# Loading raw activations behind the store of their pair, and ordering their splits and sums behind the evictions

## The chip, the cores and the metric

The program runs on one core of one Trainium2 chip. The metric is the device time of a whole run in microseconds (us), from launch to the last output, taken as the median of several runs. The engines that matter are TensorE (PE in the rows: matrix multiplies; PEld: its weight loads), VectorE (DVE), ScalarE (ACT), GpSimd (POOL) and SyncE (SP, which here issues DMAs).

## The reference

One layer of a backbone with a state-space branch, a Fourier branch and a SwiGLU feed-forward stage, for 128 context tokens and 1024 latent tokens, all in float32. The change lies in the feed-forward stage alone:

```
h2 = rmsnorm(x, p["norm2_g"]) * (1.0 + scale2) + shift2
ff = (jax.nn.silu(h2 @ p["w_ffn_gate"]) * (h2 @ p["w_ffn_up"])) @ p["w_ffn_down"]
x = x + gate2 * ff
```

The model width D is 1024 and the hidden width 2816, which is 22 tiles of 128, taken as 11 pairs p = 0 to 10. The 1152 tokens are 9 tiles of 128.

## The kernel before

**Split products.** A float32 operand is held as two parts: a rounded copy (written by an ACT cast) and the rest (source minus rounded copy, by a two-input subtraction on POOL or DVE). A product of two such operands takes three matmuls for each 128-row step. `split` (L962, L963) does this for weights; `one` (L1294, L1295) does it for activations.

**Units of the gate and up projections.** `ffn_unit(p, "g" or "u", which)` multiplies the weights of one pair of hidden tiles with the tokens of sub-batch A (5 token tiles, 320 columns a matmul), B (4 tiles, 256 columns) or both, by a Strassen-Winograd scheme of seven products, in the order Z, W, X, Y, Z, X, Y. Each letter has one PSUM bank for each sub-batch, so a letter's second use needs the first to have been evicted. Evictions run on DVE (W at L1179, X at L1182 and L1193, Y at L1185 and L1197, into `ftA` and `fstB`) and ACT (Z at L1176, Silu at L1166); POOL makes the sums of weight blocks (L1172 to L1174, L1188) and multiplications (L1168). Tiles carry the unit in their names: `YAg7AB` is bank Y of sub-batch A in the gate unit of pair 7, `wh_u2AB` a split weight block of the up unit of pair 2.

**Order of the units.** Pair 0 is done first for sub-batch A only. Pairs 1 to 10 follow, gate then up, for both sub-batches. Behind pair 2 stand the two units of pair 0 for sub-batch B ("0B", `g0B` and `u0B`). Each weight unit loads two blocks of 512 KB, into a ring `ws` of three buffers. Only the gate weights of 0B, `ws_g0B` (L1126, L1127), go into another place: the pool `pgb` under the tag `gb`, which has a single buffer.

**Raw activations.** The end of an up unit stores the pair to device memory, `ffd` (L1207). For pairs 0 to 8 the 1024 latent tokens of it come back (L1278, two loads of 512 KB) as a tile `ra`, also with the tag `gb`. `a_steps(m)` turns `ra` into the seven operands P1 to P7 that the down projection wants: four sums on DVE (L1283) and seven splits (ACT L1294, DVE L1295) into a ring `stg` of three buffers, of which each is stored as `ad` (L1297). That is eleven operations of DVE and seven of ACT for each pair. They are passed as hooks, one for each product of the units of pair p = m + 1 (pair 10 for m = 0). The program order of the hooks is only a proposal: a scheduler orders the instructions of each engine by their dependences and modelled times.

**Down projection.** It runs in blocks, first m = 0 alone, then pairs of m. Block 0 starts with a tile `A1`, again with the tag `gb`, that holds P1 and P2 of m = 0 (L1358, loaded from `ad`); P6, P5 and P7 of m = 0 stay in `stg` and are not stored. The operands of block 1 (m = 1 and 2) are loaded ahead of block 0 for four of the seven products.

**Queues.** All these loads and stores are issued by SP in one order, and each waits there for its data and its buffer.

Of the kernel before, what the change touches and what calls it, by code (L numbers as in the profile page):

```python
# [10 lines left out]
F32 = mybir.dt.float32  # L11
F32R = mybir.dt.float32r
I32 = mybir.dt.int32
AF = mybir.ActivationFunctionType
ALU = mybir.AluOpType
# [4 lines left out]
NS = 1024  # L20
# [7 lines left out]
NF = FF // 128  # L28
G, P, H = 32, 64, 16
# [32 lines left out]
def tile_flow_step(ctx: ExitStack, tc: tile.TileContext, a, o):  # L62
    nc = tc.nc
    V, S, PL, PE, SY = nc.vector, nc.scalar, nc.gpsimd, nc.tensor, nc.sync
# [723 lines left out]
    for p in range(2):  # L788
        cs_ = slice(128 * p, 128 * p + 128)
        ev, od, oo, pp = mm_tile(f"ev{p}"), mm_tile(f"od{p}"), mm_tile(f"oo{p}"), aux_tile(f"fp{p}")  # L790
# [60 lines left out]
    for q in range(4):  # L851
# [3 lines left out]
                     func=AF.Gelu_apprx_tanh)  # L855
        S.activation(out=z32[:, q, NS:TOK].rearrange("p (c s) -> p s c", s=T), in_=zt[:, :, 0:CP],
                     func=AF.Gelu_apprx_tanh)
# [22 lines left out]
    pgb = open_pool("pgb", side="right")  # L880
# [74 lines left out]
    def weight_ws(src, name, n=1024):  # L955
        st = wr.tile([128, n], F32, tag="ws", bufs=NWS, name="ws_" + name)
        SY.dma_start(out=st, in_=src)
        return st
# [140 lines left out]
    ffd = dram.tile([NF, 128, TOK], F32, tag="ffd", name="ffd")  # L1099
    psF, fsl, tmp, last_st = {}, {}, {}, []  # L1100

    BORD = {"A": "YXWZ", "B": "ZWXY"}

    def open_sub(s, pools, tpool, tag=None):
        for z in "ZWXY":
# [9 lines left out]
        fsl[s] = fs_.rearrange("p (f t e c) -> p f t e c", f=2, t=nt, e=2)  # L1115
        tmp[s] = tm_.rearrange("p (v t c) -> p v t c", v=3, t=nt)

    def ffn_unit(p, kind, which, hooks=()):
        hooks = list(hooks)
        gate_ = kind == "g"  # L1120
        src = a["w_g"] if gate_ else a["w_u"]
        nm = f"{kind}{p}{which}"
        if nm == "g0B":
            gbw = pgb.tile([128, 2048], F32, tag="gb", name="ws_" + nm)
            w0, w1 = gbw[:, 0:1024], gbw[:, 1024:2048]
            SY.dma_start(out=w0, in_=src[0])  # L1126
            SY.dma_start(out=w1, in_=src[1])  # L1127
        else:
            w0 = weight_ws(src[2 * p], nm + "0")
            w1 = weight_ws(src[2 * p + 1], nm + "1")  # L1130
        a11, a12, a21, a22 = w0[:, 0:512], w0[:, 512:], w1[:, 0:512], w1[:, 512:]
        s1 = wr.tile([128, 512], F32, tag="S1", name="s1_" + nm)
        bk = {s: {z: psF[z + s].tile([128, 512], F32, tag=z + s, name=f"{z}{s}{nm}") for z in BORD[s]}
              for s in which}
        done = set()

        def le(i):
            return V if which == "B" or which == "A" and i % 2 == 0 else PL

        def product(w, tb, z):  # L1140
            for s in which:
                tv, nt, _ = subs[s]
                ps = bk[s][z][:, 0:64 * nt].rearrange("p (t c) -> p t c", c=64)
                first = (s, z) not in done
                done.add((s, z))
                for k in range(4):
                    ks = slice(128 * k, 128 * k + 128)
                    for i, (wv, tv_) in enumerate(((0, 0), (0, 1), (1, 0))):
                        PE.matmul(ps, w[:, wv, ks], tv[:, 0:nt, tv_, tb, k, :],
                                  start=(first and k == 0 and i == 0), stop=(k == 3 and i == 2),  # L1150
                                  skip_group_check=True)
            if hooks:
                hooks.pop(0)()

        def each(fn):
            for s in which:
                nt = subs[s][1]
                b = {z: t[:, 0:64 * nt].rearrange("p (t c) -> p t c", c=64) for z, t in bk[s].items()}
                fn(s, b, tmp[s], fsl[s])

        def put(fi, e, val):
            def go(s, b, t, fs):
                v = b[val] if isinstance(val, str) else t[:, val]
                dst = fs[:, fi, :, e, :]
                if gate_:
                    S.activation(out=dst, in_=v, func=AF.Silu)  # L1166
                else:
                    (V if isinstance(val, str) else PL).tensor_tensor(dst, dst, v, ALU.mult)  # L1168
            each(go)

        h = split(a11, nm + "a11", le(0))
        PL.tensor_tensor(s1, a21, a22, ALU.add)  # L1172
        PL.tensor_tensor(a21, a21, a11, ALU.subtract)
        PL.tensor_tensor(a11, s1, a11, ALU.subtract)  # L1174
        product(h, B11, "Z")
        each(lambda s, b, t, fs: S.copy(out=t[:, 0], in_=b["Z"]))  # L1176
        h = split(a11, nm + "s2", le(1))
        product(h, T2, "W")
        each(lambda s, b, t, fs: V.tensor_tensor(t[:, 0], t[:, 0], b["W"], ALU.add))  # L1179
        h = split(a21, nm + "s3", le(2))  # L1180
        product(h, T3, "X")
        each(lambda s, b, t, fs: V.tensor_tensor(t[:, 1], t[:, 0], b["X"], ALU.subtract))  # L1182
        h = split(s1, nm + "s1", le(3))
        product(h, T1, "Y")
        each(lambda s, b, t, fs: V.tensor_tensor(t[:, 1], t[:, 1], b["Y"], ALU.add))  # L1185
        put(1, 0, 1)
        h = split(a12, nm + "a12", le(4))
        PL.tensor_tensor(a12, a12, a11, ALU.subtract)  # L1188
        product(h, B21, "Z")
        put(0, 1, "Z")  # L1190
        h = split(a22, nm + "a22", le(5))
        product(h, T4, "X")
        each(lambda s, b, t, fs: V.tensor_tensor(t[:, 2], t[:, 0], b["X"], ALU.subtract))  # L1193
        put(1, 1, 2)
        h = split(a12, nm + "s4", le(6))
        product(h, B22, "Y")
        each(lambda s, b, t, fs: V.tensor_tensor(t[:, 0], t[:, 0], b["Y"], ALU.add))  # L1197
        put(0, 0, 0)
        if not gate_:
            for s in which:  # L1200
                _, nt, c0 = subs[s]
                st_ = dict(out=ffd[2 * p:2 * p + 2, :, c0:c0 + 128 * nt].rearrange("f p c -> p f c"),
                           in_=fsl[s].rearrange("p f t e c -> p f (t e c)"))
                if p == NF // 2 - 1:
                    last_st.append(st_)
                else:
                    SY.dma_start(**st_)  # L1207

    ps1 = open_pool("psF1", space=PSUM)
    pst_ = open_pool("psT", space=PSUM, side="right")  # L1210
# [35 lines left out]
    hk, no = h2_hooks(2), (lambda: None)  # L1246
# [14 lines left out]
    pst_.release()  # L1261
    ps2 = open_pool("psF2", space=PSUM)
    open_sub("B", {z: ps2 for z in "ZWXY"}, pm0, "m0a")
    KEYS = ("P1", "P2", "P6", "P5", "P7", "P4", "P3")
    LO, HI = slice(0, 512), slice(512, 1024)
    BLK = [[0]] + [[m, m + 1] for m in range(1, 9, 2)]
    STD = [9, 10]
    ad = {m: dram.tile([7, 128, 2, 512], F32, tag=f"ad{m}", name=f"ad{m}") for m in range(STD[0])}
    stg = pm0.tile([128, 3, 2, 512], F32R, tag="m0b", name="stg")
    nstg = 0  # L1270

    def a_steps(m):
        a_ = {}

        def start():
            raw = pgb.tile([128, 2, NS], F32, tag="gb", name=f"ra{m}")
            for f in range(2):
                SY.dma_start(out=raw[:, f], in_=ffd[2 * m + f][:, 0:NS])  # L1278
                for z, h in (("L", LO), ("H", HI)):
                    a_[f"{f}{z}"] = raw[:, f, h]  # L1280

        def comb(out, x, y, op=ALU.subtract):
            V.tensor_tensor(a_[out], a_[x], a_[y], op)  # L1283

        def p6():
            comb("0H", "0H", "1H", ALU.add)
            comb("0L", "0H", "0L")

        def one(ki):
            nonlocal nstg  # L1290
            src = a_[dict(P1="0L", P2="1L", P6="0L", P7="0L", P4="1H", P5="0H", P3="1L")[KEYS[ki]]]
            st_ = stg[:, nstg % 3]
            nstg += 1
            S.copy(out=st_[:, 0], in_=src)  # L1294
            V.tensor_tensor(st_[:, 1], src, f32(st_[:, 0]), ALU.subtract)  # L1295
            if m or ki not in (2, 3, 4):
                SY.dma_start(out=ad[m][ki], in_=f32(st_))  # L1297

        def do(*fs):
            return lambda: [one(f) if isinstance(f, int) else f() for f in fs]  # L1300

        p7a, p7b = (lambda: comb("1L", "1L", "0L")), (lambda: comb("0L", "1H", "0L"))
        return [no, no, start, no, no, no, do(0), do(1), do(5), p6, do(p7a, 6), do(2), do(3), do(p7b, 4)]

    for p in range(1, NF // 2):
        hk = a_steps((p - 1) % STD[0]) if p > 1 else [no] * 14
        ffn_unit(p, "g", "AB", hk[:7])
        ffn_unit(p, "u", "AB", hk[7:])
        if p == 2:
            ffn_unit(0, "g", "B")  # L1310
            ffn_unit(0, "u", "B")


    ps2.release()
# [35 lines left out]
    def load_at(m, ki):  # L1350
        key = KEYS[ki]
        if (m, key) in AT:
# [28 lines left out]
    def load_raw(m):  # L1381
        load_w(m)
        if m in STD:
            load_a(m)
# [10 lines left out]
    def prep(m, ki):  # L1395
        key = KEYS[ki]
        w0L, w0H, w1L, w1H = raws[m]
# [240 lines left out]
    for ki in range(7):  # L1638
        prep(0, ki)
    load_w(1)  # L1640
    for ki in range(4):
        for m in BLK[1]:
            load_at(m, ki)
    load_p(0)
# [123 lines left out]
```

## Time and profile before

| what | value |
|---|---|
| runs of the kernel before | 1544.62, 1551.46 and 1552.18 us, median 1551.46 |
| time of the profiled execution | 1544.15 us |
| its span from first to last instruction | 1542.4 us |
| mean granted clock of TensorE in it | 0.981 |
| busy: PE, DVE, ACT, POOL | 95%, 60%, 37%, 42% |
| DMA, mean over the span | 158 GB/s |

The shares of busy time are averages over stages with different limits; the feed-forward stage runs from about 694 us to the end, of which pairs 1 to 10 with 0B end at 1266.0 us. A window row gives the busy time of each engine in a stretch, then the granted clock of TensorE (1.00 is 2.4 GHz, 0.50 is 1.2 GHz), the mean share of the 16 DMA engines and their rate. In a timeline row the bracket tells how long the engine sat idle ahead of the instruction and what ended that.

### The profile page before, as it was taken

To read this page: it belongs to the slowest core of one execution; us is meant where nothing else is said; L and a number is where in the kernel's file an instruction comes from. 1 tells how busy PE (TensorE), PEld (TensorE's weight loads), DVE (VectorE), ACT (ScalarE), POOL (GpSimd) and SP (SyncE) were. 2 spreads that over 40 slices of the span, in tenths; PEclk is the share of its full clock that TensorE was granted. 3 is DMA by queue.
4 is the path that set the end of the run, shared out by engine and by line. 5 is a ranking of instruction groups with operands and counts; after the bars stand their busy time and mean duration, and the time that the engine had idled before them with its cause. 6 is when DMAs were issued, how large, how long until landed. Compare 5 with 4: busy or idle time off the path is not lost. (4 is left out here: it accounts for less than half of the span.)

```text
span 1542.4 us, 24033 instructions
## 1 busy us (share of the span) xinstructions
PE 1463.8 (95%) x8999; PEld 1312.6 (85%) x8999; DVE 928.8 (60%) x1838; ACT 565.0 (37%) x1096; POOL 648.9 (42%) x606
## 2 busy tenths in 40 slices
PE   6999999999999999988999999999999998999995
PEld 3799998899967778877689999999999996888774
DVE  4647989995264335379934544335454626667778
ACT  6523334343543122355543433233342334112323
POOL 4900000000132111455587587867677781322264
PEclk9999999999999999999899999999999999999998
DMA  8343233232525643454514444443544629666423
GB/s 317 110 130 96 75 109 115 74 105 101 171 76 197 201 145 110 152 203 165 191 69 161 167 173 176 148 158 147 209 181 154 236 102 392 228 219 225 143 69 123
DMA packets 101983, 243.83 MB, mean 158 GB/s; under 512 B 15710, under 2 KB 46047, under 8 KB 101868
## 3 DMA queue, kind: packets, MB, share of 16 engines
q1 hardware_dynamic: 101868, 242.30, 44.8%
q8 instruction: 71, 1.16, 0.3%
q14 instruction: 44, 0.36, 0.1%
HBM read 172.51 MB, written 69.74 MB: 157 GB/s over the span
## 5 line engine op out<-in xcount | busy, mean ns | idle before, releaser
L94 POOL TENSOR_TENSOR wh_glu<-ws_glu,wh_glu 128x512 fp32r<-128x512 f32 x4 | 5.1, 1275 | 338.4 <-ACT wh_glu L93 338.4
L271 PE MATMUL g<-h,wh_g 128*128 128x384 f32 (+1 forms) x432 | 147.3, 341 | 0.0
L272 PE MATMUL g<-h,wh_g 128*128 128x384 f32 (+1 forms) x432 | 147.1, 341 | 0.0
L273 PE MATMUL g<-h,wh_g 128*128 128x384 f32 (+1 forms) x432 | 146.3, 339 | 0.0
L1295 DVE TENSOR_TENSOR stg<-ra,stg 128x512 fp32r<-128x512 f32 x63 | 69.9, 1112 | 44.9 <-ACT stg L1294 44.9
L272 PEld LDWEIGHTS g<-h,wh_g 128*128 128x128 f32 x432 | 81.4, 188 | 0.2 <-issue 0.2
L271 PEld LDWEIGHTS g<-h,wh_g 128*128 128x128 f32 x432 | 81.2, 188 | 0.3 <-issue 0.3
L273 PEld LDWEIGHTS g<-h,wh_g 128*128 128x128 f32 x432 | 81.2, 188 | 0.2 <-issue 0.2
L1393 POOL TENSOR_TENSOR wd<-wd,wd 128x512 f32<-128x512 f32 x25 | 35.8, 1447 | 107.1 <-DMA wd<-in_w_d 57.7
L94 POOL TENSOR_TENSOR wh_pj<-ws_pj,wh_pj 128x512 fp32r<-128x512 f32 x16 | 22.1, 1380 | 104.3 <-ACT wh_pj L93 94.6
L1294 ACT CAST stg<-ra 128x512 fp32r<-128x512 f32 x63 | 38.1, 619 | 70.2 <-DMA ra<-ffd 47.2
L1446 DVE TENSOR_TENSOR acc<-acc,U 128x1024 f32<-128x1024 f32 x34 | 41.4, 1219 | 34.8 <-PE U L1427 34.5
L963 DVE TENSOR_TENSOR wh_out<-ws_out,wh_out 128x512 fp32r<-128x512 f32 x32 | 33.8, 1071 | 23.1 <-ACT wh_out L962 23.1
L1427 PE MATMUL q<-B,A 128*128 128x512 f32 x192 | 45.6, 393 | 0.6 <-DVE acc L1446 0.4
L1427 PEld LDWEIGHTS q<-B,A 128*128 128x128 f32 x192 | 35.8, 187 | 9.6 <-DVE acc L1446 0.8
L923 DVE TENSOR_TENSOR sgc<-sgc,p 128x384 f32<-128x384 f32 x24 | 13.3, 554 | 48.4 <-PE p L106 48.4
L963 POOL TENSOR_TENSOR wh_out<-ws_out,wh_out 128x512 fp32r<-128x512 f32 x16 | 22.4, 1406 | 47.2 <-ACT wh_out L962 41.9
L977 PE MATMUL o<-wh_out,m 128*128 128x512 f32 x96 | 37.0, 413 | 4.2 <-ACT scr0b L1059 4.2
L636 DVE TENSOR_TENSOR ta<-X,Sg 128x56 f32<-128x56 f32 (+10 forms) x88 | 39.2, 445 | 1.1
L639 DVE TENSOR_TENSOR X<-X,tb 128x56 f32<-128x56 f32 (+10 forms) x88 | 39.1, 453 | 0.9
L638 DVE TENSOR_TENSOR X<-X,ta 128x56 f32<-128x56 f32 (+10 forms) x88 | 38.8, 449 | 0.2
L637 DVE TENSOR_TENSOR tb<-X,Sg 128x56 f32<-128x56 f32 (+10 forms) x88 | 38.8, 441 | 0.0
(1638 smaller groups left out, 4479.5 us busy)
## 6 DMA issues: line engine op xcount, KB each, us to landing
ad<-stg SPq DMA_DIRECT2D x60, 512.0 KB, 2.6
A<-ad SPq DMA_DIRECT2D x60, 512.0 KB, 5.9
wa<-in_w_ada SPq DMA_DIRECT2D x48, 512.0 KB, 6.2
ws_out<-in_w_out SPq DMA_DIRECT2D x24, 512.0 KB, 4.1
wd<-in_w_d SPq DMA_DIRECT2D x22, 512.0 KB, 4.5
ind<-in SPq DMA_DIRECT2D x54, 192.0 KB, 1.9
ws_g<-in_w_in SPq DMA_DIRECT2D x18, 512.0 KB, 3.5
sgc<-ind SPq DMA_DIRECT2D x48, 192.0 KB, 3.2
```

The source lines that it names most:

```text
L271: PE.matmul(ps, w[:, 0, wsl], hi, start=first, stop=False)
L272: PE.matmul(ps, w[:, 0, wsl], lo, start=False, stop=False)
L273: PE.matmul(ps, w[:, 1, wsl], hi, start=False, stop=last)
L636: V.tensor_tensor(A, src, Sc[:, 0, lv, gs].unsqueeze(1).unsqueeze(3).to_broadcast(shp), ALU.mult)
L637: V.tensor_tensor(B, src, Sg[:, :, lv, gs].unsqueeze(3).to_broadcast(shp), ALU.mult)
L638: V.tensor_tensor(dst, dst, A, ALU.add)
L639: V.tensor_tensor(dst, dst, B[:, ::-1], ALU.add)
L963: (eng or PL).tensor_tensor(w[:, 1, :], src, f32(w[:, 0, :]), ALU.subtract)
L1294: S.copy(out=st_[:, 0], in_=src)
L1295: V.tensor_tensor(st_[:, 1], src, f32(st_[:, 0]), ALU.subtract)
L1427: PE.matmul(ps, A[:, va], B[:, vb], start=(first and ti == 0 and i == 0), stop=(last and ti == n - 1 and i == 2), skip_group_check=True)
L1446: V.tensor_tensor(dst, dst, ps, ALU.add)
```

## The change

Three things change. The load of `ra` stands in program order right behind the store of its pair, in `ffn_unit`, instead of in the third hook of the next gate unit; the second weight load of an up unit is ordered behind it. Where pair 2 is concerned, it stands behind 0B, and for m = 0 it stands behind pair 9. Every hook is ordered behind the last eviction of DVE and the last one of ACT that precede it in program order. And ahead of block 0 two products' operands of block 1 are loaded, not four.

```
+    def ra_load(m):
+        ra[m] = pgb.tile([128, 2, NS], F32, tag="gb", name=f"ra{m}")
+        for f in range(2):
+            i_ = SY.dma_start(out=ra[m][:, f], in_=ffd[2 * m + f][:, 0:NS]).ins
+        ra_ins[:] = [i_]
...
-            w1 = weight_ws(src[2 * p + 1], nm + "1")
+            with tc.issue_after(ra_ins[0]) if ra_ins and not gate_ else ExitStack():
+                w1 = weight_ws(src[2 * p + 1], nm + "1")
...
             if hooks:
-                hooks.pop(0)()
+                with ExitStack() as es:
+                    for i_ in ev.values() if p else ():
+                        es.enter_context(tc.issue_after(i_))
+                    hooks.pop(0)()
+
+        def ve(*x):
+            ev["V"] = V.tensor_tensor(*x).ins
+
+        def sc(**x):
+            ev["S"] = S.copy(**x).ins
...
                 else:
                     SY.dma_start(**st_)
+            if len(which) == 2 and p < STD[0] and p != 2:
+                ra_load(p)
...
-        def start():
-            raw = pgb.tile([128, 2, NS], F32, tag="gb", name=f"ra{m}")
-            for f in range(2):
-                SY.dma_start(out=raw[:, f], in_=ffd[2 * m + f][:, 0:NS])
...
-        return [no, no, start, no, no, no, do(0), do(1), do(5), p6, do(p7a, 6), do(2), do(3), do(p7b, 4)]
+        return [no, no, no, no, no, no, do(0), do(1), do(5), p6, do(p7a, 6), do(2), do(3), do(p7b, 4)]
...
             ffn_unit(0, "u", "B")
+            ra_load(2)
+        if p == NF // 2 - 2:
+            ra_load(0)
...
-    for ki in range(4):
+    for ki in range(2):
         for m in BLK[1]:
             load_at(m, ki)
```

The evictions of W, X and Y call `ve`, those of Z call `sc`, and Silu sets `ev["S"]`.

**DVE in the gate unit of pair 7.** Before (L1182, L1185, L1193 and L1197 are evictions, L1283 sums and L1295 splits of `ra`):

```order
L1182 TENSOR_TENSOR ftA<-ftA,XAg7AB 128x320
L1295 TENSOR_TENSOR stg<-ra_10914,stg 128x512
L1182 TENSOR_TENSOR fstB<-fstB,XBg7AB 128x256
L1283 TENSOR_TENSOR ra_10914<-ra_10914 128x512
L1295 TENSOR_TENSOR stg<-ra_10914,stg 128x512
L1283 TENSOR_TENSOR ra_10914<-ra_10914 128x512
L1295 TENSOR_TENSOR stg<-ra_10914,stg 128x512
L1185 TENSOR_TENSOR ftA<-ftA,YAg7AB 128x320
L1283 TENSOR_TENSOR ra_10914<-ra_10914 128x512
L1185 TENSOR_TENSOR fstB<-fstB,YBg7AB 128x256
```

Of the change, behind the last product of the gate unit (L1172 is now every eviction of W, X and Y, L1308 a split, L1296 a sum):

```order
L1172 TENSOR_TENSOR fstB<-fstB,YBg7AB 128x256
L1308 TENSOR_TENSOR stg<-ra_10813,stg 128x512 x2
L1172 TENSOR_TENSOR ftA<-ftA,WAu7AB 128x320
L1172 TENSOR_TENSOR fstB<-fstB,WBu7AB 128x256
L1296 TENSOR_TENSOR ra_10813<-ra_10813 128x512 x2
L1172 TENSOR_TENSOR ftA<-ftA,XAu7AB 128x320
L1172 TENSOR_TENSOR fstB<-fstB,XBu7AB 128x256
L1296 TENSOR_TENSOR ra_10813<-ra_10813 128x512
L1172 TENSOR_TENSOR ftA<-ftA,YAu7AB 128x320
L1308 TENSOR_TENSOR stg<-ra_10813,stg 128x512
L1172 TENSOR_TENSOR fstB<-fstB,YBu7AB 128x256
L1308 TENSOR_TENSOR stg<-ra_10813,stg 128x512 x2
```

The first split moved from between the first evictions of X in the gate unit to the place just ahead of that unit's last two evictions, which stand just ahead of this piece. The eleven operations now spread as far as the last product of the up unit, where the seventh split stands between that product's evictions of A and B. Behind the last row here comes the multiplication by the up product Z, which frees bank Z.

**SP around 0B.** Before (`ad_7684` is `ad` of m = 1, `ra_8248` is `ra` of m = 1):

```order
L1278 DMA ra_8248<-ffd 128x1024 x2
L957 DMA ws_u0B_8756<-in_w_u 128x1024
L1297 DMA ad_7684<-stg 128x1024 x7
L1126 DMA ws_g0B<-in_w_g 128x1024
L1127 DMA ws_g0B<-in_w_g 128x1024
L957 DMA ws_u0B_8758<-in_w_u 128x1024
L957 DMA ws_g3AB_8885<-in_w_g 128x1024
L1207 DMA ffd<-fsA 128x2x640
```

Of the change (`ra_8885` is `ra` of m = 2; `ffd<-fsA` at L1229 is the store of pair 2):

```order
L957 DMA ws_u0B_8758<-in_w_u 128x1024
L1310 DMA ad_7684<-stg 128x1024 x2
L957 DMA ws_g3AB_8888<-in_w_g 128x1024
L1310 DMA ad_7684<-stg 128x1024 x4
L1229 DMA ffd<-fsA 128x2x640
L1138 DMA ws_g0B<-in_w_g 128x1024
L1139 DMA ws_g0B<-in_w_g 128x1024
L1229 DMA ffd<-fstB 128x2x512
L1127 DMA ra_8885<-ffd 128x1024 x2
L957 DMA ws_g3AB_8890<-in_w_g 128x1024
```

The loads of `ws_g0B` stood ahead of the store of pair 2; they now stand behind it, and behind the store of the seventh split of m = 1.

**SP at the end of pair 10.** Before (`ad_7683` is `ad` of m = 0, `A_12751` is the tile `A1`, `wd` are weights of the down projection):

```order
L1278 DMA ra_12360<-ffd 128x1024 x2
L957 DMA ws_g10AB_12261<-in_w_g 128x1024
L1297 DMA ad_7683<-stg 128x1024 x2
L957 DMA ws_u10AB_12491<-in_w_u 128x1024
L1297 DMA ad_7683<-stg 128x1024 x2
L1358 DMA A_12751<-ad_7683 128x1024 x2
L1207 DMA ffd<-fsA 128x2x640
L1207 DMA ffd<-fstB 128x2x512
L957 DMA ws_u10AB_12493<-in_w_u 128x1024
L1378 DMA wd_12752<-in_w_d 128x1024
```

Of the change:

```order
L1127 DMA ra_12259<-ffd 128x1024
L1229 DMA ffd<-fstB 128x2x512
L957 DMA ws_u10AB_12493<-in_w_u 128x1024
L1394 DMA wd_12752<-in_w_d 128x1024
L1310 DMA ad_7683<-stg 128x1024
L1394 DMA wd_12754<-in_w_d 128x1024
L1310 DMA ad_7683<-stg 128x1024 x2
L1394 DMA wd_12787<-in_w_d 128x1024
L1310 DMA ad_7683<-stg 128x1024
L1374 DMA A_12751<-ad_7683 128x1024 x2
```

The load of `A1` stood ahead of the store of pair 9; it is now behind the weights of the down projection and the last store of m = 0, and its buffer is that of `ra` of m = 0, which is read up to the last split of pair 10.

## Rows read from the trace of the kernel before

**Rows 1.** The page: the span, and the first part, busy time.

```profile
span 1542.4 us, 24033 instructions
PE 1463.8 (95%) x8999; PEld 1312.6 (85%) x8999; DVE 928.8 (60%) x1838; ACT 565.0 (37%) x1096; POOL 648.9 (42%) x606
```

**Rows 2.** The waits of PE, 740 to 1266 us: total, times, longest.

```profile
PE YAg7AB L1149 <- DVE ftA L1185: 3.3, 1, 3.3
PE YAg9AB L1149 <- DVE ftA L1185: 2.4, 1, 2.4
PE YAg6AB L1149 <- DVE ftA L1185: 2.4, 1, 2.4
PE XAu9AB L1149 <- DVE ftA L1182: 2.0, 1, 2.0
PE YAg5AB L1149 <- DVE ftA L1185: 1.8, 1, 1.8
```

**Rows 3.** Windows: 0B with pair 3, then pairs 4, 7 and 10.

```profile
870.35:937.63 67.28, 64.95 (x506) 64.19 (x505) 31.13 (x53) 25.90 (x53) 53.03 (x45) 1.00 0.40 144
937.63:982.01 44.38, 44.38 (x338) 44.38 (x337) 19.27 (x33) 16.26 (x33) 30.50 (x25) 1.00 0.49 181
...
1075.42:1126.10 50.68, 47.34 (x338) 47.17 (x337) 20.41 (x33) 16.24 (x33) 37.27 (x32) 0.93 0.42 159
...
1221.59:1266.00 44.41, 44.41 (x339) 44.41 (x338) 11.18 (x26) 12.41 (x26) 37.97 (x35) 1.00 0.29 100
```

**Rows 4.** Timelines of SP, ACT, DVE and PE in the gate unit of pair 7.

```profile
1084.76 0.81 SPq L1278 DMA_DIRECT2D ra<-ffd  x2
...
1090.34 0.62 ACT L1294 CAST stg<-ra 128x512 fp32r<-128x512 f32 x1 [6.93 <-DMA ra<-ffd]
...
1090.99 1.51 DVE L1295 TENSOR_TENSOR stg<-ra,stg 128x512 fp32r<-128x512 f32 x1 [6.72 <-ACT stg L1294]
...
1097.31 0.47 DVE L1185 TENSOR_TENSOR ftA<-ftA,YAg7AB 128x320 f32<-128x320 f32 x1
...
1097.93 3.54 PE L1149 MATMUL YAg7AB<-TA,wh_g7ABs 128*128 128x320 f32 x12 [3.34 <-DVE ftA L1185]
```

**Rows 5.** Windows behind that wait, and around another wait of PE.

```profile
1097.90:1101.50 3.60, 3.57 (x14) 3.60 (x15) 2.71 (x5) 3.43 (x8) 0.40 (x1) 0.50 0.61 245
...
685.40:689.55 4.15, 0.00 (x0) 0.00 (x0) 4.15 (x8) 0.51 (x2) 1.44 (x1) 0.76 0.09 20
689.55:693.90 4.35, 4.35 (x10) 3.47 (x11) 4.35 (x10) 1.76 (x4) 2.98 (x3) 0.50 0.56 222
```

**Rows 6.** Timelines of SP, ACT, POOL and PE around the start of 0B.

```profile
851.21 0.45 SPq L1126 DMA_DIRECT2D ws_g0B<-in_w_g  x1
...
855.81 0.62 ACT L962 CAST wh_g0Ba<-ws_g0B 128x512 fp32r<-128x512 f32 x1 [1.53 <-DMA ws_g0B<-in_w_g]
...
862.29 1.15 ACT L962 CAST wh_g0Bs<-ws_g0B 128x512 fp32r<-128x512 f32 x2 [5.86 <-POOL ws_g0B L1174]
...
857.08 1.29 POOL L1172 TENSOR_TENSOR s_g0B<-ws_g0B 128x512 f32<-128x512 f32 x1 [2.21 <-DMA ws_g0B<-in_w_g]
...
871.75 1.56 PE L1149 MATMUL WBg0B<-TB,wh_g0Bs 128*128 128x256 f32 x12
```

**Rows 7.** Timelines of SP and POOL: one weight load of 512 KB.

```profile
1108.80 0.33 SPq L957 DMA_DIRECT2D ws_g8AB<-in_w_g  x1
...
1112.36 1.29 POOL L1172 TENSOR_TENSOR s_g8AB<-ws_g8AB 128x512 f32<-128x512 f32 x1 [2.33 <-DMA ws_g8AB<-in_w_g]
```

**Rows 8.** Timeline of PE in blocks 0 and 1.

```profile
1265.99 2.97 PE L1427 MATMUL U<-B0P,A 128*128 128x512 f32 x12
...
1298.64 0.50 PE L1427 MATMUL Y<-B1P,A 128*128 128x512 f32 x1 [1.21 <-ACT B1P L1346]
```

**Rows 9.** A window at the start of the down projection.

```profile
1266.00:1286.00 20.00, 19.63 (x86) 15.59 (x84) 8.09 (x8) 8.88 (x11) 5.20 (x5) 1.00 1.00 372
```

**Rows 10.** The tile stg: its splits on DVE (ns, minimum, median, maximum), its stores.

```profile
L1295 DVE TENSOR_TENSOR stg<-ra,stg x63: 676/694/1794, 837.1 to 1219.3; 128x512 fp32r<-128x512 f32 x63
...
DMA to landing us min/median/max: 2.6/2.6/3.9
```

More of the change, by code (lines that the diff above doesn't have):

```diff
@@ L1102, in tile_flow_step @@
     BORD = {"A": "YXWZ", "B": "ZWXY"}
+    ev, ra, ra_ins = {}, {}, []
     def open_sub(s, pools, tpool, tag=None):
@@ L1116, in open_sub @@
         tmp[s] = tm_.rearrange("p (v t c) -> p v t c", v=3, t=nt)
+    KEYS = ("P1", "P2", "P6", "P5", "P7", "P4", "P3")
+    LO, HI = slice(0, 512), slice(512, 1024)
+    BLK = [[0]] + [[m, m + 1] for m in range(1, 9, 2)]
+    STD = [9, 10]
+    def ra_load(m):
[3 more added lines that the diff above has]
+        ra_ins[:] = [i_]
     def ffn_unit(p, kind, which, hooks=()):
@@ L1165, in go @@
                 if gate_:
-                    S.activation(out=dst, in_=v, func=AF.Silu)
+                    ev["S"] = S.activation(out=dst, in_=v, func=AF.Silu).ins
                 else:
@@ L1175, in ffn_unit @@
         product(h, B11, "Z")
-        each(lambda s, b, t, fs: S.copy(out=t[:, 0], in_=b["Z"]))
+        each(lambda s, b, t, fs: sc(out=t[:, 0], in_=b["Z"]))
         h = split(a11, nm + "s2", le(1))
         product(h, T2, "W")
-        each(lambda s, b, t, fs: V.tensor_tensor(t[:, 0], t[:, 0], b["W"], ALU.add))
+        each(lambda s, b, t, fs: ve(t[:, 0], t[:, 0], b["W"], ALU.add))
         h = split(a21, nm + "s3", le(2))
         product(h, T3, "X")
-        each(lambda s, b, t, fs: V.tensor_tensor(t[:, 1], t[:, 0], b["X"], ALU.subtract))
+        each(lambda s, b, t, fs: ve(t[:, 1], t[:, 0], b["X"], ALU.subtract))
         h = split(s1, nm + "s1", le(3))
         product(h, T1, "Y")
-        each(lambda s, b, t, fs: V.tensor_tensor(t[:, 1], t[:, 1], b["Y"], ALU.add))
+        each(lambda s, b, t, fs: ve(t[:, 1], t[:, 1], b["Y"], ALU.add))
         put(1, 0, 1)
@@ L1192, in ffn_unit @@
         product(h, T4, "X")
-        each(lambda s, b, t, fs: V.tensor_tensor(t[:, 2], t[:, 0], b["X"], ALU.subtract))
+        each(lambda s, b, t, fs: ve(t[:, 2], t[:, 0], b["X"], ALU.subtract))
         put(1, 1, 2)
@@ L1196, in ffn_unit @@
         product(h, B22, "Y")
-        each(lambda s, b, t, fs: V.tensor_tensor(t[:, 0], t[:, 0], b["Y"], ALU.add))
+        each(lambda s, b, t, fs: ve(t[:, 0], t[:, 0], b["Y"], ALU.add))
         put(0, 0, 0)
@@ L1263, in tile_flow_step @@
     open_sub("B", {z: ps2 for z in "ZWXY"}, pm0, "m0a")
[L1264 to L1267, printed above, removed]
     ad = {m: dram.tile([7, 128, 2, 512], F32, tag=f"ad{m}", name=f"ad{m}") for m in range(STD[0])}
@@ L1272, in a_steps @@
     def a_steps(m):
-        a_ = {}
-        def start():
-            raw = pgb.tile([128, 2, NS], F32, tag="gb", name=f"ra{m}")
-            for f in range(2):
-                SY.dma_start(out=raw[:, f], in_=ffd[2 * m + f][:, 0:NS])
-                for z, h in (("L", LO), ("H", HI)):
-                    a_[f"{f}{z}"] = raw[:, f, h]
+        a_ = {f"{f}{z}": ra[m][:, f, h] for f in range(2) for z, h in (("L", LO), ("H", HI))}
         def comb(out, x, y, op=ALU.subtract):
```

## The prediction

> **What bounds the kernel now.** The page says that PE is busy 95% of the span [rows 1]. So the question is not who is slow on average but where PE stands still. For the feed-forward stage I read the list of PE's waits first: in pairs 5 to 9 it waits for DVE's eviction of a bank, 1.8 to 3.3 us each time, 11.9 us in five waits [rows 2]. Then the windows, pair by pair: pair 4 has no wait and takes 44.38 us, in which PE is busy throughout; pair 7 takes 50.68 us at a granted clock of 0.93 [rows 3]. The reader is to see that 44.38 us is the floor of a pair, and that a wait costs more than its length. Pair 7 lies 6.3 us above the floor, but its wait is 3.34 us. The rest is clock: right behind the wait the granted clock is 0.50, which is 1.2 GHz, and elsewhere 4.15 us without a matmul are followed by 4.35 us at 0.50 [rows 5]. At half the clock 4.35 us do the work of 2.2, so a restart costs 2.2 to 3.0 us on top of the idle time.
>
> Then the timeline, to see why DVE was late in pair 7 [rows 4]. SP issues the raw load at 1084.76; the first cast finds its data at 1090.34; DVE, idle for 6.72 us, starts the first split at 1090.99. Three sums and three splits have been put between the first X evictions and the Y eviction, which therefore comes at 1097.31. PE wanted that bank 3.34 us before 1097.93. DVE was idle first and then had everything at once.
>
> **What the change takes away.** From 937.63 to 1266.00 there are seven pairs in 328.37 us [rows 3]. Seven floors are 7 x 44.38 = 310.7. The excess is 17.7 us, and it consists of these waits and the slow clock behind them. In the new order no split stands between evictions that a next product waits for until the gate unit's sixth product is evicted, and the load is issued a whole gate unit earlier, so it has landed. I take the 17.7 us as gone, with 12 as the lower end, if one or two waits stay.
>
> Does DVE keep up? The densest place is the up unit. A product takes 44.38 / 14 = 3.17 us, an eviction at most 0.47 [rows 4], a split between 0.68 and 1.79 [rows 10]. I take the worst, 1.77 each. Behind product W come two evictions and two sums, 0.94 + 3.54 = 4.48 us, so DVE is 1.3 us late at X. Behind X: 1.3 + 0.94 + 1.77 = 4.0, so 0.85 late at Y. Behind Y an eviction, a split, an eviction, two splits: 0.85 + 0.94 + 5.3 = 7.1 us after Y's end. The multiplication that frees bank Z starts then and ends some 7.6 us after Y's end. The next unit wants that bank three products after Y's end, at 9.5. About 2 us are left, at the worst price of every operation; so the cost here is nothing.
>
> A rule speaks against this. The Trainium skill (GPSIMD Engine Reference, Specifications) lists GpSimd's SBUF interfaces as shared with VectorE, with contention for VectorE instructions that have two SBUF inputs; splits and sums are of that kind, and they move beside POOL's work. The trace agrees, since one shape takes 676 to 1794 ns [rows 10]. By the rule all eleven would pay, which is the case worked out above, and it still fits; the rule's own outcome is the second rival.
>
> The up unit's second weight load now stands behind two raw loads of 512 KB. At 372 GB/s [rows 9] these take 2.8 us. It is wanted at the start of the up unit, half a pair (22 us) later, so I cost it at nothing; without that cover it would be 2.8 us a pair.
>
> **First loss: the start of 0B.** The gate weights of 0B share the single buffer with the raw activations. Before, all splits of m = 1 were early, the load was issued at 851.21, and 0B started at 870.35 without a wait [rows 3, 6]. Now the seventh split of m = 1 stands behind the A eviction of the last product of the up unit of pair 2. Call the end of that unit E. The A half of the last product ends 1.4 us before E; an eviction of 0.47 and a split of 0.7 to 1.8 put the release of the buffer at E - 0.2 to E + 0.9, and I take E + 0.4. SP then still issues the store of that split and the store of pair 2 ahead, some 0.4 us each (0.45 for one issue, [rows 6]), so the load is issued at E + 1.3. From issue to the first cast took 4.6 us, from issue to the first POOL sum 5.87 [rows 6]. So product Z starts at about E + 6.7, and POOL starts its three sums at E + 7.2, which are 3.9 us at 1.29 each. A cast of 0.6 and a little for the semaphores follow, and W starts at E + 11.9. Before, it started at 871.75, which is E + 1.4. Behind W thirteen products of B remain, at 1.40 each (871.75 - 870.35), which is 18.2. With 2.5 us for the slow clock, 0B ends at E + 32.6, and pair 3 adds 44.4: 77.0 us against 67.28 [rows 3]. The 67.28 held 3.2 us over the floor of 64.1 (44.38 x 4/9 for 0B, and 44.38); that goes too, since pair 3's weights have time enough. **Loss 9.7 us.** If the load lands in 3.56 us, as an undisturbed one did [rows 7], and SP has nothing ahead, it is about 5 to 6; if the buffer comes free late by a further 3 us, 13.
>
> **Second loss: block 0.** P1 and P2 of m = 0 come through the tile A1. Before, its load was long done and block 0 followed without a wait at 1265.99 [rows 8]. Now it waits for the last split of pair 10, by the same working 0.4 to 0.9 us after the end T of that pair. A load takes 3.56 us [rows 7], so the first matmul starts at about T + 4.2, and the restart costs 2.6. Some comes back: in block 1 PE waits for operands anyway, 1.21 us once [rows 8], at a time when the DMA engines are full [rows 9], and a later PE waits less for them. On the other side 1 MB of A1 now falls into that full time (2.8 us at 372 GB/s), while 2 MB of block 1's operands move out of it. I give back 1.5 us. **Loss 5.3 us**, 3 to 8. Loading two products ahead, not four, is a part of this term alone.
>
> **The sum** is -17.7 + 9.7 + 5.3 = -2.7 us. The profiled execution took 1544.15 us (span 1542.4, [rows 1], and 1.75 around it), so the same execution comes to 1541.4. But of the three runs of before one lies at that level and two lie 7 to 8 us above it; the median is 7.3 above the profiled time. Where the median of three runs of the changed kernel falls is open by that much. I take the middle, 1541.4 + 3.6 = **1545.0 us**, which is 0.4% below 1551.46. A measurement of this kernel can tell about 0.5%, 7.8 us, from no change: faster is below 1543.7, slower above 1559.2.
>
> **The rivals.**
> First, **cheap restarts**: the two new waits lie at their lower ends, 5.5 and 3. That is -17.7 + 8.5 = -9.2, and 1538.5 us by the same middle. For it: the 3.56 us of an idle queue [rows 7]. Against: at 0B three POOL sums stand in a row.
> Second, on the other side, **DVE too late after all**: the three splits behind Y in the up unit need a free buffer of the ring of three, and a store takes 2.6 us to land [rows 10]. If each of the last two waits for such a store, the bunch grows by more than the 2 us that are left, and PE waits at the start of each of the nine units that follow, some 2 us. It decides from 2 us on. That gives -2.7 + 18 = +15.3, 1563 us. The rule of the Trainium skill on shared interfaces (GPSIMD Engine Reference, Specifications) points the same way, since it makes the splits the longest exactly where they are bunched. Against: DVE at the worst price still fits.
> Third, **dear restarts**: 13 and 8 at the two places, -17.7 + 21 = +3.3, 1551 us, no change.
> Fourth, **the change does not do what it says**: the raw loads come no earlier, since SP is in order and something ahead of them waits, and the splits end as late as ever. Then the 17.7 us stay and the losses come on top: +15, 1563 us. Against: the store of the pair is all that stands ahead of the load.
>
> **How the numbers follow.** Chances: the forecast 0.50, cheap restarts 0.20, dear restarts 0.17, DVE too late 0.08, no earlier load 0.05. Because of the two levels of the runs, a little under half of the forecast's chance (0.22) falls below 1543.7, and nearly all of cheap restarts (0.19): faster 0.41. Slower are the second and fourth rival but for a little, 0.11. The rest, 0.48, is the same. The range 1533 to 1556 holds the forecast, the cheap and the dear restarts at either level of the runs but for their ends, and leaves out the two slow rivals.
>
> **What would show it.** Right: no wait for `ftA` or `fstB` in the gate units of pairs 5 to 9, each of pairs 4 to 10 close to 44.4 us; a gap of PE of about 6.7 us ahead of `ZBg0B` and one of 4 to 5 ahead of `WBg0B`, with a granted clock of 0.50 behind; 0B and pair 3 together at about 77 us from the end of the last Y product of pair 2; a gap of about 4 us ahead of the first U of block 0. Wrong: waits at bank Z at the start of the units behind each pair's splits; a gap ahead of `ZBg0B` under 3 or over 10 us; a raw load that is issued in the gate unit's third product or later; or waits on weights in the up units, which I have costed at nothing.

## The result and the profile after

The changed kernel is slower. Five runs of it took 1560.15 to 1564.09 us (median 1561.44), five of before 1544.62 to 1552.18 (median 1548.83): a ratio of 1.0082, with a 95% interval of 1.0059 to 1.0105. The forecast was 1545.0 with a range of 1533 to 1556, so the time lies outside it, on the side to which I gave 0.11.

The profiled execution of the changed kernel took 1564.09 us, with a span of 1562.3 (before: 1542.4, [rows 1]). Its stages come out of the start times of PE's first matmuls. E is the end of pair 2, T the end of pair 10, each of them the start of the next matmul less PE's wait for it:

| stage (us) | before | after | difference | forecast |
|---|---|---|---|---|
| start to E | 870.35 | 873.89 | +3.5 | 0 |
| 0B and pair 3 | 67.28 | 78.59 | +11.3 | +9.7 |
| pairs 4 to 10 | 328.37 | 317.99 | -10.4 | -17.7 |
| T to the end | 276.41 | 291.83 | +15.4 | +5.3 |

The first line is no effect of the change: 3.4 us of it lie ahead of pair 1 (which begins at 778.20 and 781.57), where the instructions of each engine stand in the same order in both kernels, and that stage varies from run to run (last section). The other three lines add up to +16.3. The medians differ by 12.6; the profiled execution of after is the slowest of its five, and that of before is at the low end of its runs.

The waits of PE in the changed kernel from 600 to 1300 us (total, times, longest), those of the stages in question:

```profile
PE U L1443 <- DMA A<-ad: 10.2, 1, 10.2
PE ZBg0B L1162 <- ACT wh_g0Ba L962: 7.6, 1, 7.6
...
PE WBg0B L1162 <- ACT wh_g0Bs L962: 2.4, 1, 2.4
...
PE WAu7AB L1162 <- POOL wh_u7ABs L963: 0.8, 1, 0.8
PE WAu8AB L1162 <- POOL wh_u8ABs L963: 0.8, 1, 0.8
...
PE WAu8AB L1162 <- ACT wh_u8ABs L962: 0.7, 1, 0.7
PE WAu7AB L1162 <- ACT wh_u7ABs L962: 0.6, 1, 0.6
```

All five waits on `ftA` of [rows 2] are gone, as forecast. In their place stand the two gaps that I had priced, at 0B and ahead of block 0, and a third kind that I had costed at nothing: product W of the up units of pairs 7 and 8 waits for split weights.

The windows of the changed kernel: 0B with pair 3, pairs 7 and 8, the gap ahead of block 0, and what follows it.

```profile
873.89:952.48 78.59, 68.12 (x506) 67.15 (x505) 37.69 (x58) 29.12 (x58) 57.37 (x46) 0.93 0.39 136
...
1086.20:1132.60 46.40, 44.99 (x336) 44.50 (x337) 21.02 (x34) 15.94 (x35) 36.02 (x29) 1.00 0.47 173
1132.60:1180.65 48.05, 46.51 (x338) 46.05 (x337) 22.44 (x37) 17.10 (x36) 37.45 (x31) 0.96 0.47 178
...
1270.47:1280.68 10.21, 0.01 (x1) 0.03 (x1) 4.61 (x9) 2.19 (x5) 9.40 (x10) 0.67 0.25 87
1280.68:1286.00 5.32, 5.32 (x16) 4.28 (x17) 0.00 (x0) 2.27 (x3) 3.11 (x3) 0.67 1.00 393
```

Pair 8 is 3.7 us above its floor of 44.38 with waits of 1.5; its clock is 0.96, so the rest is again the restart. In the gap ahead of block 0 POOL is busy for 9.40 of 10.21 us. POOL had no part in the forecast of that gap, so this is the first sign that something else is late there.

**The gap at 0B.** SP, ACT, PE and POOL in the changed kernel (timelines):

```profile
873.65 0.32 SPq L1310 DMA_DIRECT2D ad<-stg  x1
874.38 0.37 SPq L1229 DMA_DIRECT2D ffd<-fsA  x1
874.80 0.51 SPq L1138 DMA_DIRECT2D ws_g0B<-in_w_g  x1
...
880.84 0.62 ACT L962 CAST wh_g0Ba<-ws_g0B 128x512 fp32r<-128x512 f32 x1 [8.35 <-DMA ws_g0B<-in_w_g]
...
881.51 3.29 PE L1162 MATMUL ZBg0B<-TB,wh_g0Ba 128*128 128x256 f32 x12 [7.62 <-ACT wh_g0Ba L962]
887.17 0.50 PE L1162 MATMUL WBg0B<-TB,wh_g0Bs 128*128 128x256 f32 x2 [2.38 <-ACT wh_g0Bs L962]
```

It is the chain of the forecast, link by link: the store of the seventh split, the store of pair 2, then the load, issued at E + 0.9 (forecast E + 1.3); Z at E + 7.6 (6.7) and W at E + 13.3 (11.9). The load took 6.0 us from issue to the first cast, where the row I used had 4.6 [rows 6].

**The up weights.** SP, POOL and PE around the up unit of pair 7, which begins its product Z at 1108.46:

```profile
1097.36 0.37 SPq L1229 DMA_DIRECT2D ffd<-fstB  x1
1100.46 0.83 SPq L1127 DMA_DIRECT2D ra<-ffd  x2
1101.38 0.38 SPq L957 DMA_DIRECT2D ws_u7AB<-in_w_u  x1
...
1107.68 1.29 POOL L1194 TENSOR_TENSOR s_u7AB<-ws_u7AB 128x512 f32<-128x512 f32 x1 [6.59 <-DMA ws_u7AB<-in_w_u]
...
1112.41 0.56 PE L1162 MATMUL WAu7AB<-TA,wh_u7ABs 128*128 128x320 f32 x2 [0.62 <-ACT wh_u7ABs L962]
```

Read from above: the raw load can't start before the store of its pair has landed, 3.1 us after its issue; the up weights follow the raw load, and land 6.3 us later; three POOL sums, a cast and a split follow. Pair 7 began at 1086.20, so the weights were issued 15.2 us into a pair that wants them split 25 us into it. Before, the same load was issued 7.8 us into pair 7, which began at 1075.42, and the raw load of [rows 4] 2.8 us after the store that it reads back. SP before:

```profile
1081.99 0.38 SPq L1207 DMA_DIRECT2D ffd<-fstB  x1
1083.24 0.35 SPq L957 DMA_DIRECT2D ws_u7AB<-in_w_u  x1
```

**The gap ahead of block 0.** The chain that ended last in the changed kernel, 1258 to 1281 us (start, length, what):

```profile
1258.53 5.98 DMA ad<-stg
...
1265.13 0.61 ACT stg L1307
...
1273.06 1.60 POOL wd L1409
1274.68 0.05 ACT B0P L1362
...
1275.82 0.53 ACT stg L1307
1276.37 0.82 DVE stg L1308
1277.22 3.32 DMA A<-ad
...
1280.68 4.62 PE U L1443 x12
```

The last link is the one I forecast: the load of A1 is issued when the last split has freed the buffer, and lands 3.3 us later. But that split ends at 1277.19, which is T + 6.7, not T + 0.4 to 0.9. ACT has one order, and ahead of the last cast of `stg` stand casts of the down weights, which wait for POOL's sums of them. ACT's timeline has two waits, the first for a store that frees one of the three buffers of `stg` (5.98 us in the chain above), the second for POOL:

```profile
1264.61 1.14 ACT L1307 CAST stg<-ra 128x512 fp32r<-128x512 f32 x2 [6.84 <-DMA ad<-stg]
...
1274.68 1.14 ACT L1362 CAST B0P<-wd 128x512 fp32r<-128x512 f32 x2 [7.37 <-POOL wd L1409]
```

### The profile page after: what moved, and what is told of

Its sections match the earlier page's. It is cut to its first block, busy times and chain, and to the rows that moved or that the text cites. A ratio compares the mean times of both kernels' runs of the same rounds, so it can differ in the third digit from the quotient of the medians.

```text
span 1562.3 us, 24032 instructions
## 1 busy us (share of the span) xinstructions
PE 1473.0 (94%) x8999; PEld 1318.6 (84%) x8999; DVE 937.5 (60%) x1838; ACT 563.9 (36%) x1096; POOL 662.9 (42%) x606
## 5 line engine op out<-in xcount | busy, mean ns | idle before, releaser
L1308 DVE TENSOR_TENSOR stg<-ra,stg 128x512 fp32r<-128x512 f32 x63 | 79.9, 1279 | 88.3 <-ACT stg L1307 88.0
L923 DVE TENSOR_TENSOR sgc<-sgc,p 128x384 f32<-128x384 f32 x24 | 13.3, 554 | 48.4 <-PE p L106 48.4
L1190 POOL TENSOR_TENSOR fsA<-fsA,ftA 128x320 f32<-128x320 f32 x33 | 34.2, 1037 | 13.6 <-DVE ftA L1172 13.6
L962 ACT CAST wh_out<-ws_out 128x512 fp32r<-128x512 f32 x48 | 28.3, 615 | 30.2 <-PE o L979 20.3
(1550 smaller groups left out, 4528.2 us busy)
```

## The experiments

My theory after this reading: three separate places, of which the third, the up weights, also makes POOL late at the end of pair 10 and so lengthens the second gap. Rivals: POOL is simply too busy; the queue on SP makes the gaps, not the shared buffer; or saved waits come back as a lower clock. Each kernel below is the changed kernel with the edit shown. Ratios are to runs of before on the same chip; the last three columns are stages of the profiled execution, as above.

| kernel | median | ratio [95%] | 0B, pair 3 | pairs 4-10 | T to end |
|---|---|---|---|---|---|
| before | | | 67.28 | 328.37 | 276.41 |
| changed | 1561.44 | 1.0082 [1.0059, 1.0105] | 78.59 | 317.99 | 291.83 |
| e1 w1 free | 1548.60 | 0.9986 [0.9970, 1.0002] | 78.53 | 310.82 | 285.26 |
| e2 pair 2 free | 1550.73 | 0.9989 [0.9969, 1.0010] | 67.65 | 318.60 | 289.22 |
| e3 pair 10 free | 1557.51 | 1.0042 [1.0023, 1.0062] | 78.57 | 316.56 | 285.30 |
| e4 all three | 1527.94 | 0.9848 [0.9818, 0.9878] | 65.14 | 310.65 | 276.57 |
| e5 = e4, w1 tied | 1543.44 | 0.9955 [0.9941, 0.9969] | 65.58 | 316.16 | 286.08 |
| e6 load only | 1550.33 | 1.0006 [0.9991, 1.0021] | 67.49 | 329.88 | 279.24 |
| e7 order only | 1532.61 | 0.9882 [0.9861, 0.9902] | 65.22 | 310.66 | 279.27 |
| e8 = e4, four ahead | 1528.83 | 0.9865 [0.9847, 0.9884] | 64.74 | 310.66 | 278.74 |
| e9 A1 apart | 1555.17 | 1.0042 [1.0028, 1.0055] | 78.52 | 315.39 | 283.59 |
| e10 = e9 and e1, e2 | 1532.91 | 0.9891 [0.9866, 0.9916] | 65.04 | 310.82 | 280.97 |
| e11 0B in ring | 1550.86 | 1.0011 [0.9995, 1.0027] | 68.16 | 314.41 | 289.09 |
| e12 = e11 and e1, e3 | 1530.11 | 0.9879 [0.9863, 0.9894] | 67.97 | 310.65 | 275.08 |

**e1.** The up weights are not tied.

```
-            with tc.issue_after(ra_ins[0]) if ra_ins and not gate_ else ExitStack():
-                w1 = weight_ws(src[2 * p + 1], nm + "1")
+            w1 = weight_ws(src[2 * p + 1], nm + "1")
```

> The changed kernel, except that the up unit's second weight load is not ordered behind the raw load. Theory (three separate new waits, one of them on the up weights in pairs 7 and 8): no wait at WAu7 and WAu8, pairs 7 and 8 at 44.4 to 45 us instead of 46.4 and 48.1, about 5.5 us less than the changed kernel, so some 7 us above before; 0B and block 0 unchanged (78.7 us; a gap of 10.2 us). Rival (POOL is too busy with the sums anyway): WAu7 and WAu8 wait as before, within 1 us of the changed kernel.

The pairs went as expected, 44.38 us each (pair 10: 44.54). But the kernel gained 15 us on the changed one (0.0096 of 1550), not 5.5, because the gap ahead of block 0 shrank too. PE's waits in e1:

```profile
PE ZBg0B L1161 <- ACT wh_g0Ba L962: 7.9, 1, 7.9
PE U L1442 <- DMA A<-ad: 4.1, 1, 4.1
```

The gap is now 4.1 us, and in DVE's timeline the last split ends at T + 0.5 (T is 1262.44): the figures that the forecast had for it.

```profile
1262.11 0.85 DVE L1307 TENSOR_TENSOR stg<-ra,stg 128x512 fp32r<-128x512 f32 x1 [0.54 <-ACT stg L1306]
```

**e2 and e3.** The hooks of pair 2, or of pair 10, are not ordered behind evictions.

```
-                    for i_ in ev.values() if p else ():
+                    for i_ in ev.values() if p not in (0, 2) else ():
...
+                    for i_ in ev.values() if 0 < p < NF // 2 - 1 else ():
```

> The changed kernel, except that the hooks of pair 2 are not ordered behind the evictions, so that the single buffer comes free early for the gate weights of 0B. Theory (the late release of that buffer makes the gap): no gap ahead of the first product of 0B, 0B with pair 3 at 64 to 68 us instead of 78.7, about 11 us less than the changed kernel, so 1 to 2 us above before. Rival (the queue: the loads of the gate weights are late because of the stores ahead of them on SP, whatever the buffer): the gap stays over 4 us.

> The changed kernel, except that the hooks of pair 10 are not ordered behind the evictions, so that the buffer of the tile A1 comes free before the end of pair 10. Theory (late release makes the gap of 10.2 us ahead of block 0, and the slow clock behind it costs the rest): no gap ahead of block 0, from the end of pair 10 to the end 277 us instead of 291.8, about 13 us less than the changed kernel, so about equal to before; pair 10 may get one wait of up to 3 us on an eviction. Rival (A1 is late because the weights of the down projection stand ahead of it): a gap of 4 us or more stays.

e2 did what its theory said: 67.65 us, 11 less than the changed kernel. In e3 the gap ahead of block 0 is gone, but the stage gained only 6.5 us, since a new wait ends 10 us behind its start. PE and ACT in e3:

```profile
1283.31 5.15 PE L1443 MATMUL U<-B0P,stg 128*128 128x512 f32 x12 [4.54 <-ACT acc L1460]
...
1281.73 0.62 ACT L1362 CAST B0P<-wd 128x512 fp32r<-128x512 f32 x1 [3.91 <-POOL fsA L1190]
1282.25 1.92 ACT L1460 COPY acc<-U 128x1024 f32<-128x1024 f32 x2
```

PE waits for ACT to empty a bank; ACT has the copy behind a cast of down weights that waits for POOL, which is late with the up unit. So freeing the buffer moved the wait, and what was late was POOL.

**e4 and e5.** e4 is e1, e2 and e3 together; e5 is e4 with the tie put back.

> The three edits together: the up weights not ordered behind the raw load, and the hooks of pairs 2 and 10 not ordered behind the evictions. Theory (three separate places, which add up): some 28 to 30 us less than the changed kernel, 13 to 17 us under before, a ratio near 0.990. Rival (the saved waits come back as lower clock or other waits): less than 8 us under before.

> The fourth kernel with one part put back: the up unit's second weight load is again ordered behind the raw load; hooks of pairs 2 and 10 stay free. Theory (this tie costs both in pairs 7 to 9 and, by making POOL and ACT late in pair 10, at the start of the down projection): waits at WAu7 to WAu9, 4 to 6 us in pairs 7 to 10, and some 5 us between the start of block 0 and that of block 1; about 10 us more than the fourth kernel, a ratio near 0.992. Rival (the tie costs only its own waits): 4 to 6 us more, a ratio near 0.988.

e4 is the version that beats both kernels, by 1.5% against before. From pair 2 to T, PE waits once, in all:

```profile
PE ZBg0B L1161 <- ACT fstB L1174: 0.2, 1, 0.2
```

Its gain is above what I wrote down (1.0082 - 0.9848 is 36 us, I had 28 to 30), as that of e1 was. e5 settles the tie: by the ratios it costs 0.0107 of 1550, some 17 us, where I had written about 10. In the stages that is 5.5 in pairs 4 to 10 and 9.5 behind T, where the wait for ACT's copy of e3 is back with 4.4 us. Some 3.4 of the 9.5 are slow clock that e7 and e8, without the tie, have as well (last section).

**e6 and e7.** e6 has the new place of the load alone (tie off, no hook ordered); e7 the order alone (e4 with the load back in the third hook).

```
-                    for i_ in ev.values() if p else ():
+                    for i_ in ():
...
+        def start():
+            ra_load(m)
...
+        return [no, no, start, no, no, no, do(0), do(1), do(5), p6, do(p7a, 6), do(2), do(3), do(p7b, 4)]
```

> The change's load place alone: raw loads behind the store of their pair, the up weights not tied, no hook ordered behind evictions, two products' operands ahead of block 0. Theory (DVE's order makes the waits, not the time of the load): waits on ftA evictions in pairs 5 to 9 of 8 us or more in total, a ratio to before of 0.995 to 1.003. Rival (the load was late, as the timeline of before suggests): these waits are gone, a ratio near 0.987.

> The fourth kernel with the raw loads put back into the third hook of the next gate unit, so only the order behind the evictions is new (pairs 2 and 10 free). Theory: the same as the fourth kernel within 3 us, a ratio of 0.983 to 0.987. Rival (the early load is a part of the gain): a ratio above 0.990, with waits on evictions or on the raw loads in pairs 4 to 10.

The load place alone gives nothing: the waits of before are back in e6, 11.8 us in five.

```profile
PE YAg8AB L1161 <- DVE ftA L1171: 3.3, 1, 3.3
PE YAg7AB L1161 <- DVE ftA L1171: 2.4, 1, 2.4
PE XAu9AB L1161 <- DVE ftA L1171: 2.4, 1, 2.4
PE YAg5AB L1161 <- DVE ftA L1171: 2.3, 1, 2.3
...
PE YAg6AB L1161 <- DVE ftA L1171: 1.4, 1, 1.4
```

SP's timeline of e6 says why. Pair 7 begins at 1077.64:

```profile
1083.63 0.38 SPq L1228 DMA_DIRECT2D ffd<-fstB  x1
1084.89 0.35 SPq L957 DMA_DIRECT2D ws_u7AB<-in_w_u  x1
1086.42 0.81 SPq L1127 DMA_DIRECT2D ra<-ffd  x2
```

The raw load starts 8.8 us into the pair. Before it was 9.3 (1084.76 - 1075.42, [rows 3, 4]): the store was the limit all along, not the place in the program. e7's pairs 4 to 10 are those of e4 to 0.01 us. Its ratio is a little above my range and 5 us behind that of e4, where I had written 3 at most; their intervals overlap, and in the profiled executions the difference sits behind T.

**e8.** e4 with four products' operands of block 1 ahead.

> The fourth kernel with four products' operands of block 1 loaded ahead of block 0, as before, instead of two. Theory (the loads move inside a stretch in which the DMA engines are full, so little changes): within 3 us of the fourth kernel. Rival (the two products' loads delay the weights of block 1): 4 us more or better by as much in the stretch from the start of block 0 to the end.

No difference that these runs tell (0.9865 against 0.9848).

**e9 and e10.** P1 and P2 of m = 0 go into the ring of the other operands.

```
-    A1 = pgb.tile([128, 2, 2, 512], F32R, tag="gb", name="A1")
...
-        AT[m, key] = A1[:, ki] if m == 0 and ki < 2 else a_new(f"A{m}_{ki}")
+        AT[m, key] = a_new(f"A{m}_{ki}")
```

> The changed kernel with only this edit: P1 and P2 of m = 0 are loaded into the ring of the other operands, not into the buffer of the raw activations. Theory (the gap of 10.2 us ahead of block 0 is the wait for that buffer, which the last split of pair 10 frees): the gap falls to 1 to 3 us, since the loads then wait only for the store of the second split and their place behind the fourth store on SP; but the down weights stay late, so 5 us come back between blocks 0 and 1, as in the third kernel. Rival (P1 and P2 themselves are stored late): the gap stays over 5 us.

> Up weights not tied, hooks of pair 2 free, hooks of pair 10 ordered, and P1 and P2 of m = 0 in the ring. Theory: with the buffer apart nothing delays block 0, so no gap over 1 us ahead of it and the same time as the fourth kernel within 3 us, a ratio of 0.983 to 0.988. Rival (the late splits of pair 10 delay the operands that stay in their staging buffers, or the stores): a gap of 2 us or more, a ratio above 0.988.

Both missed: gaps of 4.2 and 2.8 us are left, and in e9 the 5 us that I had expected did not come back (from the first U of block 0 to that of block 1 it is 22.2 us, 21.6 in the changed kernel, 26.8 in e3). SP's waits in e10 name what I had overlooked:

```profile
SPq L1372 <- PE YAu10AB L1161: 7.9, 1, 7.9
```

The ring is free only when PE has read the activations of the up unit for the last time, at the end of pair 10. So this ring gives A1 no earlier place; whether another would, no run here shows. What did work is to free the shared buffer early (e4). The splits of pair 10 are not shown to delay anything else in e10.

**e11 and e12.** The gate weights of 0B go into the ring of the other weights; e12 adds the edits of e1 and e3.

```
-        if nm == "g0B":
+        if nm == "none":
```

> The changed kernel with only this edit: the gate weights of 0B go into the ring of the other weights, not into the buffer of the raw activations; the hooks of pair 2 stay ordered. Theory (the single buffer makes the gap at 0B, not the order of the hooks): no gap over 2 us ahead of 0B, 0B with pair 3 at 66 to 70 us instead of 78.7, 8 to 12 us less than the changed kernel, a ratio of 1.000 to 1.003. Rival (the loads stand behind the stores of the splits on SP in any case): a gap over 4 us stays.

> Gate weights of 0B in the ring of the other weights, up weights not tied, hooks of pair 10 free, hooks of pair 2 ordered. Theory: as the fourth kernel within 3 us, a ratio of 0.983 to 0.988. Rival (with three buffers the ring makes the weights of pair 3 late): 4 us more or worse, with waits on weights at the start of pair 3.

With the hooks of pair 2 still ordered the gap at 0B is gone (68.16 us), so it was the buffer, not the queue or the order as such. In e12 small waits in 0B and pair 3 (1.3 and 0.9 us on split weights, 0.7 on ACT's `fstB`) leave this stage 2.8 us behind e4. Its ratio is at the edge of what I wrote for it.

## Why the prediction was wrong

**The gain was right.** I took 17.7 us of waits and slow clock in pairs 4 to 10 as gone. In e4 and e7 the stage is 310.65 and 310.66, 17.7 under 328.37. That DVE keeps up at its worst price held too: the median split grew from 694 ns [rows 10] to 1397 in the changed kernel, and no wait on an eviction came of it in pairs 4 to 10. The rule on shared interfaces (the Trainium skill, GPSIMD Engine Reference, Specifications: contention with VectorE instructions that have two SBUF inputs) agrees with the longer splits: before, the 25 splits without a POOL instruction beside them took 676 to 694 ns and the other 38 a median of 1717, and in the changed kernel all 63 run beside one. That they would cost time, as my second rival had it, did not happen. One reading of the trace was off: ahead of the late Y eviction in [rows 4] DVE had two sums and three splits, not three and three; no term of the sum rests on it. The splits' row in the changed kernel:

```profile
L1308 DVE TENSOR_TENSOR stg<-ra,stg x63: 685/1397/1784, 850.1 to 1276.4; 128x512 fp32r<-128x512 f32 x63
```

**The step that failed** is "It is wanted at the start of the up unit, half a pair (22 us) later, so I cost it at nothing." I had put the raw load at the pair's beginning, and so wrote that it "is issued a whole gate unit earlier". In the trace of before the load was issued 9.3 us into the pair, because the store must land first, and nothing in the change moves the store. It was even later in the changed kernel, 14.3 us. The fourth rival was true as to the load, and wrong only in what followed from it, since the order alone removes the waits. Tied to the load, the up weights were issued 15.2 us into pair 7, and what I had at nothing costs some 15 us: 15 by e1 against the changed kernel, 17 by e5 against e4, of which some 3 may be the slow clock.

**The second loss, 5.3 us, was right for itself and wrong in this kernel.** Without the tie, e1, the last split ends at T + 0.5 and the gap is 4.1 us, against T + 0.4 to 0.9 and 4.2 forecast. With it, the gap is 10.2 and the stage 15.4 longer. I had followed DVE's order to the last split and left out ACT's, in which that split's cast stands behind casts that wait for POOL. In e1 the order of DVE, ACT and POOL there is the same, and ACT waits 6.8 us for the same sums; but the up weights of pair 10 were issued 39.0 us ahead of T (at 1223.49), in the changed kernel 32.5 (at 1237.98). So it is not the order that makes the gap longer, but how late POOL is. Of the 15.4, 10.2 are the gap, 1.65 are the first product U at a low clock (4.62 us against 2.97, [rows 8]), and some 3.4 are two later stretches of the changed kernel at a clock of 0.83, which the kernel before does not have:

```profile
1315.00:1325.00 10.00, 8.51 (x28) 6.29 (x29) 8.58 (x10) 2.91 (x5) 6.57 (x4) 0.83 1.05 401
1480.00:1490.00 10.00, 8.05 (x28) 5.82 (x27) 6.48 (x7) 2.43 (x4) 4.41 (x3) 0.83 0.34 105
```

These two go with no edit (last section), so they look like scatter. e1 has them too, so of the 8.9 us by which its stage is longer some 5.5 are left, an estimate, against the 5.3 of the forecast. The 1.5 us that I gave back are not to be seen by themselves: a gap of 4.1 and a first product that is 1.6 longer are already 5.7.

**The first loss, 9.7 us, measured 11.3**: the load of 0B's weights took 1.4 us longer than the row I priced it by, and the rest of the chain held.

**The comparison of levels.** I forecast against a median of 1551.46; the five runs give 1548.83, and e1 to e12 compare with medians of 1549.4 to 1551.1. That is inside what I had left open.

So the changed kernel holds a gain of 17.7 us and three costs: about 11 at 0B, some 15 from the tie, and 9 behind T that are there without the tie, of which some 3.4 are that slow clock. e4 keeps the gain and drops the costs.

## What to carry to other kernels

When a load reads back what the kernel has stored, its earliest time is the landing of the store: read that in the trace before you move the load in the program, since a queue that is in order makes everything tied behind it as late. A buffer that two stages share hands the lateness of the one to the other: delaying its last reader by a few operations made two gaps, and freeing just those two places, with the tie gone, kept the whole gain. When you cost a wait at a buffer, follow the order of each engine that feeds its last reader (here ACT, behind POOL), not only that of the engine that reads it.

## What was not expected of the hardware

**Lateness fed itself.** In the changed kernel the up weights were issued 8.5 us into pair 4 (961.00 - 952.48), 10.8 into pair 5, 14.1 into pair 6 and 15.2 into pair 7. Late weights make POOL late, POOL multiplies the pair's result last, so the store and the next raw load are late, and with them the next weights. It grew no further in pairs 8 and 9 (14.9 and 14.4), and without the tie, in e1, it stays at 5.1 to 5.9 in pairs 4 to 9. Pairs 4 and 5 took 44.38 us, the floor, pair 6 took 44.96, and PE's waits began only in pair 7, so a trace of the first pairs would have shown little.

**Much of the scatter arises ahead of this stage.** In the profiled executions, pair 1 begins between 777.8 us (e6) and 785.5 (e3), with the same instructions ahead of it. The runs of before spread over 14 us (1543.99 to 1558.02), so this is about half of it, which is why stages were compared here, not spans.

**After the same short pauses the clock is not the same.** Ahead of 1287 us PE waits 1.2 and 0.55 us for DVE in e4 and in e7, and between 1450 and 1460 us 1.6 us for DVE's `acc` in both. The windows of e4 and then of e7:

```profile
1285.00:1290.00 5.00, 3.87 (x14) 2.67 (x15) 4.91 (x8) 1.85 (x4) 1.96 (x2) 1.00 1.04 397
1450.00:1460.00 10.00, 7.70 (x31) 5.66 (x31) 7.73 (x8) 2.49 (x4) 6.44 (x4) 1.00 0.49 146
```

```profile
1285.00:1290.00 5.00, 4.35 (x12) 2.90 (x11) 4.92 (x7) 1.76 (x3) 2.81 (x2) 0.67 1.05 400
1450.00:1460.00 10.00, 8.07 (x27) 5.80 (x26) 6.47 (x6) 1.87 (x3) 5.30 (x4) 0.83 0.34 105
```

The granted clock stays at 2.4 GHz in the one and falls for a while in the other, which costs 0.33 of 5 us and 0.17 of 10, some 3.4 us together. That covers the 2.7 us by which e7 is behind e4 after T. Both stretches are there in seven of the fourteen traces (the changed kernel, e1, e3 and e5 to e8) and neither in the other seven, among them e2, which keeps the gap of 10 us. What decides between the two, no run here shows.
